# Hybrid trunk on one core: two banks in turn for the weighted values, the head mixes written two slots later, and an end stage laid out anew

## The chip, the core and the metric

The kernel runs on one core of a Trainium2 chip. The core has five engines that work side by side, each through its own list of instructions in order: PE (TensorE, the matrix unit), DVE (VectorE), ACT (ScalarE), POOL (GpSimd) and SP (SyncE, which here issues every DMA transfer). An engine stops where its next instruction waits for another engine or for a transfer, and everything behind that instruction stops with it. The metric is the device time of one execution in microseconds (us); lower is better.

## The reference

Two residual layers on x (2048 tokens by 1024), then an RMSNorm. Layer 0 is gated linear attention. Layer 1, which the change touches, is dilated attention: six heads of width 128, each in three groups with other windows and dilations, mixed by a softmax over the groups' log-sums. Both layers also attend to 256 memory tokens.

```python
for i in range(DEPTH):                                   # DEPTH = 2
    h = rmsnorm(x, norm_w[i])
    mix, q_mem, gate = gla_mixer(...) if i % 2 == 0 else dilated_mixer(h, w_in_b[0])
    mem_o = memory_attention(q_mem, mem_n, w_memkv[i])
    branch = jnp.concatenate([mix, mem_o], axis=-1) * jax.nn.silu(gate)
    x = x + branch @ w_out[i]
return rmsnorm(x, final_norm_w)

# dilated_mixer: DIL_GROUPS = ((128, 1), (512, 4), (2048, 16)), 6 heads of 128
for g, (window, dil) in enumerate(DIL_GROUPS):
    q, k, v = ...                                        # h @ w_in, rope on q and k
    o, lse = dilated_group(q, k, v, window, dil)         # softmax(q k) v, and its log-sum
wts = jax.nn.softmax(jnp.stack(lses, axis=0), axis=0)    # over the three groups
o = jnp.einsum('gbth,gbthd->bthd', wts, jnp.stack(outs, axis=0))
```

## The kernel before

Most operands are split into a high and a low half (two f16 or two fp32r numbers), and the helper `mm3` (lines 180 to 182) multiplies them in three matmuls: L180, L181 and L182 are these three, whoever calls. A tile of PSUM, the memory into which PE writes, is called a bank (128x512 f32). There are eight: `ps_mm` 2, `ps_tr` 2, `ps_g` 2, `ps_o` 1, `ps_x` 1. A pool with two banks hands them out in turn, and a new owner waits until the last reader of the old one is done. `mm_bank` gives out `ps_mm` and `ps_x` in turn.

The attention of layer 1 is a loop over 144 slots (`for s in range(NS)`): 18 units, which are the 6 heads in 3 groups each, by 8 slots. In each slot PE runs, in the order of the program text (`manual_schedule` for PE):

- the scores of slot s-10 into a `ps_g` bank (`att_scores`). DVE masks them and takes the maximum (L1223), DVE makes the exponent's bias (L1227), ACT takes the exponential, POOL splits it in halves, and SP turns the result round by a DMA (`pt<-ph`, L175);
- the weighted values of slot s-13 (`att_pv`, called `pv`): `pt` times `v`. Two slots fill one bank, `ob`; at the next even slot a new one is taken. DVE empties the full bank into `osb` (L1261; into a tile `rw` in the last head);
- the projections of q and k of the next unit (24 matmuls 128x512, `proj_t`). ACT and DVE (L1174, L1175) empty their banks, and every fourth slot the rotary embedding follows, at whose end eight DVE copies (L1193) write q and k, which the scores read.

Once per head, 35 slots after its begin, its three groups are mixed: `att_stats` turns the statistics round (a transpose into `ps_tr`, DVE copy L1275 to `stT`, DMA to `std`), `prep_load` and `prep_mix` work out the mixing weights (`nm`, `dn`; L1299 to L1309) and write them to memory (`fd`). For each of four chunks of 512 tokens `item_og` loads the group outputs (`og`) and the gate (`sg`), `item_fb` loads the weights broadcast to all partitions (`fb`, 768 KB; one tile, so that a chunk's load waits for the mix before), and `item_mix` multiplies and adds (DVE L1341, L1347, L1348, L1350; POOL L1339, L1344) and stores the branch (`brd`, L1352). The weights and values of the next unit (`v<-vd`, 1 MB, L1165) are loaded by the same SP queue.

The end stage is `for x in range(14)`: the last ten slots of scores and thirteen of weighted values, the last gate projection in eight halves (`gate_half`, 12 matmuls 128x512), the mix of head 5 chunk by chunk, and the splits of the output weights and of the branches (`wo_split`, ACT L1427 and DVE L1428). Each of 16 blocks of 128 tokens is then multiplied with the output weights. `load_b` loads and splits a block's seven finished eighths of the branch, `f_main(d, P1)` and `f_main(d, P2)` multiply these with the left and the right 512 columns, `f_fin` adds the eighth that holds head 5 (from `b5s[c]`, the mixed chunk c, which serves blocks 4c to 4c+3) and DVE adds the residual (L1532), which empties the bank. `f_mm` is both one behind the other. Three `f_main` stand inside the end stage: block 0 both sides, block 1 left.

The order of DVE, ACT, POOL and SP is not that of the text: a planner works it out from the dependences when the program is built. PE follows the text here.

Of the kernel before, what the change touches and what calls it, by code (L numbers as in the profile page):

```python
# [35 lines left out]
def trunk(ctx, tc, a, out):  # L36
# [1209 lines left out]
    def att_pv(hd, step):  # L1246
        u, vt = hd["u"], hd["v"]
        pth, ptl, runs = hd["pv"].pop(step)
        j2 = step % 2
        if j2 == 0:  # L1250
            hd["ob"] = bank(ps_o)
        ob = hd["ob"]
        for r_, (kb, sl, n, j) in enumerate(runs):
            x, y = (kb // 4, kb % 4) if u[1] == 0 else (kb % 4, kb // 4)
            cs = slice(sl * P, (sl + n) * P)
            mm3(ob[:, j * P:(j + n) * P], vt[:, x, 0, y], vt[:, x, 1, y], pth[:, cs], ptl[:, cs],
                j2 == 0 and r_ == 0, j2 == 1 and r_ == len(runs) - 1)
        if j2 == 1:
            j4 = step // 2
            osb = tl(*((bk, [P, 512], F32, "rw") if hd["ns"] < 16 and j4 % 2 else (gk, [P, 512], F32, "osb")))  # L1260
            V.tensor_copy(osb, ob)  # L1261
            if hd["ns"] == 16:
                SY.dma_start(o_d[hd["h"]][u[1]][:, j4 * 512:(j4 + 1) * 512], osb)
            else:
                hd["osb"][j4] = osb
# [108 lines left out]
    for s in range(NS):  # L1374
# [31 lines left out]
        if 0 <= h < 5:  # L1406
            step = 4 if h < 4 else 2
            if x == 0:
                att_stats(hds[3 * h + 2], 0)
                preps[h] = prep_load(h)  # L1410
            if x == 1:
                prep_mix(preps.pop(h))
            y, z = divmod(x - 5, step)
            if 0 <= y < 4 and z == 0:
                item_mix(*items.pop(y))
            y, z = divmod(x - 3, step)
            if 0 <= y < 4 and z == 0:
                items[y] = (item_og(h, y), item_fb(h, y))
# [26 lines left out]

    raws = {0: wo_raw(0, tl(stg, [P, KT, 256], F32, "stg"))}
    wo0 = [tl(wp, WSH, F32R, "w") for _ in range(4)]
    its, fbs, pre, b5s = {}, {}, {}, {}
    for x in range(14):
# [4 lines left out]
        c, odd = divmod(x - 4, 2)  # L1454
        if 0 <= c < 4 and not odd:
            att_stats(last, c)
        if x < 8:
            gate_half(x)
# [18 lines left out]
        if x in (5, 6):  # L1477
            ks = slice(4 * (x - 5), 4 * (x - 4))
            wo_split(raws[1][:, ks], wo1[0][:, ks], wo1[1][:, ks])
        if x == 5:  # L1480
# [3 lines left out]
        if x == 7:  # L1484
# [9 lines left out]
            def load_b(p_):  # L1494
                xt = tl(fp, [P, D], F32, "x")
                br = tl(f0, [P, KT - 1, P], F32, "br")
                for k0, k1 in ((0, 5), (6, 8)):
                    o = 0 if k0 == 0 else 5
                    SY.dma_start(br[:, o:o + k1 - k0], br_d[p_ // 4][:, p_ % 4, k0:k1])
                SY.dma_start(xt, x1v[p_])  # L1500
                bhl = tl(f0, [P, 2, KT - 1, P], F32R, ("bhl0", "bhl1")[p_ % 2])
                wo_split(br, bhl[:, 0], bhl[:, 1])
                return dict(p=p_, x=xt, b=bhl, ss=tl(sp, [P, 4], F32, "ss4"), n=0, t={},
# [9 lines left out]
            def f_main(d, parts):  # L1513
                t = mm_bank()
# [39 lines left out]
        if x in (8, 9):  # L1554
            fs[x - 8] = load_b(x - 8)
        if x in (9, 10, 11, 12):
            j, kh = divmod(x - 9, 2)
            ks = slice(4 * kh, 4 * kh + 4)
            wo_split(raws[2 + j][:, ks], *(w[:, ks, j * 256:(j + 1) * 256] for w in wo2))
        if x == 9:  # L1560
            f_main(fs[0], P1)
        if x == 10:
            f_main(fs[1], P1)
        if x == 12:
            f_main(fs[0], P2)
            fs[2] = load_b(2)
    for p_ in range(NB):
        d = fs.pop(p_)
        if p_ > 1:
            f_mm(d, P1)  # L1570
        if p_ + 1 < NB and p_ > 1:
            fs[p_ + 1] = load_b(p_ + 1)
        if p_ == 0:
            f_fin(d, P1)
            f_fin(d, P2)
        elif p_ == 1:
            f_fin(d, P1)
            f_mm(d, P2)
# [5 lines left out]
        f_end(p_, d, D if p_ + 1 < NB else 512)  # L1584

# [54 lines left out]
```

## Time and profile before

| | us |
|---|---|
| median of 3 runs (lowest, highest) | 2668.18 (2666.09, 2670.78) |
| profiled execution, its own time | 2676.5 |
| its span, first to last instruction | 2674.7 |
| PE busy in it | 2532.0 (95%) |
| DVE, ACT, POOL busy | 1610.2, 1342.8, 562.6 |
| mean granted TensorE clock | 0.979 of full speed |

The profiled execution lies 0.31% above the median, and 1.8 us of it lie around the span. PE is busy for all but 142.7 us of the span, so a wait of PE is the thing to look for. In a row of the timeline the first number is the start, the second the length, then engine, line, operation, output and inputs, and in square brackets the idle time of the engine before the instruction and what ended it.

### The profile page before, as it was taken

The page shows a single profiled execution, that of the slowest core. Times are in us where ns is not written, and L with a number is a line of the kernel's source. Part 1 is how long each engine was busy: PE and PEld are TensorE (multiplying, and loading weights), DVE is VectorE, ACT ScalarE, POOL GpSimd, SP SyncE. Part 2 cuts the span into 40 slices and gives each one's busy share as a digit, 9 for nine tenths or more (in the row PEclk, how much of TensorE's full clock was granted, in tenths as well). Part 3 has the DMA queues.
Part 4 walks back from the last instruction along what each step waited for, and adds up shares of the span by engine and source line. Part 5 has one row for each costly group of instructions (what it writes and reads, how often), then busy time and mean ns, then how long its engine had stood idle before and what let it go on. Part 6 is the DMA issues. An engine that isn't in the chain of part 4 may idle for free. (4 is left out here: it accounts for less than half of the span.)

```text
span 2674.7 us, 45223 instructions
## 1 busy us (share of the span) xinstructions
PE 2532.0 (95%) x17137; PEld 1698.7 (64%) x17137; DVE 1610.2 (60%) x3595; ACT 1342.8 (50%) x2957; POOL 562.6 (21%) x471
## 2 busy tenths in 40 slices
PE   7999999899999899999999999899998998987799
PEld 6879999788889644544444455454454544544798
DVE  7445444656866656655645556767767676676543
ACT  6356444544444446556545555454554645545122
POOL 0000000001210134555541122222223222232200
PEclk9999999899999999999999999999999999998899
DMA  6242112334433535777664144654646446476542
GB/s 207 83 130 90 66 52 77 119 101 111 145 97 100 162 124 142 173 171 186 158 171 154 46 87 102 174 140 124 158 116 174 123 118 159 118 172 178 167 155 100
DMA packets 528493, 349.72 MB, mean 131 GB/s; under 512 B 355650, under 2 KB 467732, under 8 KB 525588
## 3 DMA queue, kind: packets, MB, share of 16 engines
q1 hardware_dynamic: 528276, 346.84, 47.5%
q8 instruction: 134, 2.20, 0.3%
q14 instruction: 83, 0.68, 0.1%
HBM read 185.74 MB, written 95.86 MB: 105 GB/s over the span
## 5 line engine op out<-in xcount | busy, mean ns | idle before, releaser
L180 PE MATMUL ps_mm<-h2T,w 128*128 128x512 f16 x1112 | 426.9, 384 | 1.2 <-ACT c L947 1.2
L181 PE MATMUL ps_mm<-h2T,w 128*128 128x512 f16 x1112 | 426.1, 383 | 0.0
L182 PE MATMUL ps_mm<-h2T,w 128*128 128x512 f16 x1112 | 426.0, 383 | 0.0
L180 PE MATMUL ps_mm<-w,hT 128*128 128x256 f16 (+1 forms) x1408 | 389.4, 277 | 3.0 <-DVE ws L123 1.1
L181 PE MATMUL ps_mm<-w,hT 128*128 128x256 f16 (+1 forms) x1408 | 388.4, 276 | 0.0
L182 PE MATMUL ps_mm<-w,hT 128*128 128x256 f16 (+1 forms) x1408 | 387.1, 276 | 0.4 <-DVE hT L384 0.4
L182 PEld LDWEIGHTS <-w 128*128 128x128 f16 x1952 | 192.8, 99 | 237.8 <-issue 12.3
L181 PEld LDWEIGHTS <-w 128*128 128x128 f16 x1952 | 192.9, 99 | 222.8 <-issue 18.5
L180 PEld LDWEIGHTS <-w 128*128 128x128 f16 x1952 | 193.0, 99 | 215.2 <-issue 9.7
L174 POOL TENSOR_TENSOR ph<-pm,ph 128x512 f16<-128x512 f32 (+2 forms) x144 | 144.9, 1006 | 615.2 <-ACT ph L173 429.9
L1232 ACT ACTIVATE pm<-pm,st,cols 128x256 f32<-128x256 f32 (+1 forms) x288 | 156.4, 544 | 172.5 <-DVE st L1227 171.3
L180 PE MATMUL ps_x<-h2T,w 128*128 128x512 f16 x552 | 212.7, 385 | 3.5 <-ACT h2T L701 1.8
L181 PE MATMUL ps_x<-h2T,w 128*128 128x512 f16 x552 | 212.5, 385 | 1.4 <-DVE h2T L702 1.4
L182 PE MATMUL ps_x<-h2T,w 128*128 128x512 f16 x552 | 212.5, 385 | 0.0
L174 POOL TENSOR_TENSOR stg<-mp,stg 128x512 f16<-128x512 f32 x16 | 18.6, 1161 | 753.2 <-DMA ogd<-og 457.3
L180 PEld LDWEIGHTS <-hT 128*128 128x128 f16 x1408 | 139.6, 99 | 24.6 <-issue 5.4
L181 PEld LDWEIGHTS <-hT 128*128 128x128 f16 x1408 | 139.5, 99 | 23.0 <-issue 4.2
L1223 DVE CUSTOM_DVE_ANT_0 pm<-ps_g,mw 128x256 f32<-128x256 f32 (+1 forms) x288 | 93.5, 360 | 99.1 <-PE ps_g L182 98.2
L182 PEld LDWEIGHTS <-hT 128*128 128x128 f16 x1408 | 140.1, 99 | 18.6 <-DVE hT L384 0.7
L1171 ACT ACTIVATE rx<-ps_mm 32x512 f32<-32x512 f32 x96 | 56.2, 585 | 136.8 <-DVE k L1193 89.1
L180 PE MATMUL ps_o<-pt,v 128*128 128x128 f16 (+1 forms) x384 | 76.5, 230 | 48.9 <-DVE osb L1261 43.0
L181 PE MATMUL ps_g<-k,q 128*128 128x256 f16 (+1 forms) x288 | 69.3, 249 | 14.1 <-DVE k L1193 14.1
(463 smaller groups left out, 6034.1 us busy)
## 6 DMA issues: line engine op xcount, KB each, us to landing
stg<-in_w_in_b SPq DMA_DIRECT2D x80, 256.0 KB
v<-vd SPq DMA_DIRECT2D x18, 1024.0 KB
fb<-fd SPq DMA_DIRECT2D x24, 768.0 KB
od<-osb SPq DMA_DIRECT2D x68, 256.0 KB
og<-od SPq DMA_DIRECT2D x68, 256.0 KB
x<-in_x SPq DMA_DIRECT2D x32, 512.0 KB
stg<-in_w_in_b SPq DMA_DIRECT2D x24, 512.0 KB
vd<-vo SPq DMA_DIRECT2D x48, 256.0 KB
```

Of the source, the lines that this page charges most:

```text
L174: G.tensor_tensor(out=lo, in0=src, in1=hi, op=ALU.subtract)
L180: PE.matmul(o, sh, mh, start=first, stop=False)
L181: PE.matmul(o, sh, ml, start=False, stop=False)
L182: PE.matmul(o, sl, mh, start=False, stop=last)
L1171: A.activation(out=X[r0 + 32 * j:r0 + 32 * j + 32, :], in_=ts[j][0:32, :], func=AF.Copy)
L1223: V.tensor_tensor_reduce(out=pm[:, at:at + w * P], in0=s[:, at:at + w * P], in1=masks["mw" if w == 2 else "mf"], scale=1.0, scalar=NEG, op ...
L1232: A.activation(out=p_, in_=p_, func=AF.Exp, scale=sc, bias=st[:, jc + jj:jc + jj + 1], accum_out=st[:, ns + jc + jj:ns + jc + jj + 1])
```

## The change

Three things are done.

1. `att_pv` takes its bank from `ps_o` and from `ps_tr` in turn, instead of always from the one of `ps_o`. `ps_tr` keeps its other users: the transposes of `att_stats` and of `pair_norm`, a norm once per unit.
2. For heads 0 to 3 the calls of `item_og`, `item_fb` and `item_mix` stand two slots later in the text (first load in slot 5 of a head's mix instead of 3, first mix in 7 instead of 5; the step stays 4). For head 4, whose step is 2, nothing changes.
3. In the end stage the gate halves run in steps 0 to 5 (two, two, then one each) instead of 0 to 7. The statistics of head 5 stand one step earlier. The rotary tables, no longer needed, take the branch loads of blocks 0 and 1 from step 1 on (`load_br`). The output weights' splits stand one or two steps earlier, and the split branches of the blocks turn through three tiles. Five `f_main` stand inside the stage instead of three: block 0 left (step 7), block 1 left (9), block 0 right (11) and block 1 right (12) into `ps_g` banks, block 2 left (13). In the closing loop blocks are loaded three ahead.

```diff
--- before.py
+++ after.py
@@ -1248,7 +1248,7 @@
         pth, ptl, runs = hd["pv"].pop(step)
         j2 = step % 2
         if j2 == 0:
-            hd["ob"] = bank(ps_o)
+            hd["ob"] = bank((ps_o, ps_tr)[step // 2 % 2])
         ob = hd["ob"]
         for r_, (kb, sl, n, j) in enumerate(runs):
             x, y = (kb // 4, kb % 4) if u[1] == 0 else (kb % 4, kb // 4)
@@ -1410,10 +1410,10 @@
                 preps[h] = prep_load(h)
             if x == 1:
                 prep_mix(preps.pop(h))
-            y, z = divmod(x - 5, step)
+            y, z = divmod(x - 3 - step, step)
             if 0 <= y < 4 and z == 0:
                 item_mix(*items.pop(y))
-            y, z = divmod(x - 3, step)
+            y, z = divmod(x - 1 - step, step)
             if 0 <= y < 4 and z == 0:
                 items[y] = (item_og(h, y), item_fb(h, y))
 
@@ -1443,6 +1443,11 @@
         if hf == 1:
             gate_silu(gt.pop(c), c)
 
+    def load_br(p_):
+        for k0, k1 in ((0, 5), (6, 8)):
+            o = 0 if k0 == 0 else 5
+            SY.dma_start(brs[p_ % 2][:, o:o + k1 - k0], br_d[p_ // 4][:, p_ % 4, k0:k1])
+
     raws = {0: wo_raw(0, tl(stg, [P, KT, 256], F32, "stg"))}
     wo0 = [tl(wp, WSH, F32R, "w") for _ in range(4)]
     its, fbs, pre, b5s = {}, {}, {}, {}
@@ -1451,11 +1456,20 @@
             scores(NS - 10 + x)
         if x < 13:
             pv(NS - 13 + x)
-        c, odd = divmod(x - 4, 2)
+        if x == 7:
+            f_main(fs[0], P1)
+        if x == 9:
+            f_main(fs[1], P1)
+        for y in ((0, 1), (2, 3), (4,), (5,), (6,), (7,))[x] if x < 6 else ():
+            gate_half(y)
+        c, odd = divmod(x - 3, 2)
         if 0 <= c < 4 and not odd:
             att_stats(last, c)
-        if x < 8:
-            gate_half(x)
+        c, odd = divmod(x - 4, 2)
+        if x == 1:
+            brs = [t[:, 0:(KT - 1) * P].rearrange("p (k n) -> p k n", k=KT - 1) for t in rope]
+            for y in range(2):
+                load_br(y)
         if 0 <= c < 4:
             if not odd:
                 pre[c] = prep_load(5, c)
@@ -1474,14 +1488,14 @@
         if x == 2:
             raws[1] = wo_raw(1, tl(stg, [P, KT, 256], F32, "stg"))
             wo1 = [tl(qp, [P, KT, 256], F32R, nm) for nm in ("q", "k")]
-        if x in (5, 6):
-            ks = slice(4 * (x - 5), 4 * (x - 4))
+        if x in (4, 5):
+            ks = slice(4 * (x - 4), 4 * (x - 3))
             wo_split(raws[1][:, ks], wo1[0][:, ks], wo1[1][:, ks])
-        if x == 5:
+        if x == 4:
             raws[2] = wo_raw(2, tl(vp, [P, KT, 256], F32, "v"))
         if x == 6:
             raws[3] = wo_raw(3, tl(stg, [P, KT, 256], F32, "stg"))
-        if x == 7:
+        if x == 5:
             ch.close()
             f0 = c4.enter_context(pool("f0", 1, "right"))
             fp = c4.enter_context(pool("fp", 3, "right"))
@@ -1491,16 +1505,15 @@
             fw = tl(wp, [P, D], F32, "w")
             SY.dma_start(fw, bcast_row(a["final_norm_w"], D))
 
-            def load_b(p_):
+            bhls = [tl(f0, [P, 2, KT - 1, P], F32R, f"bhl{y}") for y in range(2)]
+
+            def load_b(p_, br=True):
+                if br:
+                    load_br(p_)
                 xt = tl(fp, [P, D], F32, "x")
-                br = tl(f0, [P, KT - 1, P], F32, "br")
-                for k0, k1 in ((0, 5), (6, 8)):
-                    o = 0 if k0 == 0 else 5
-                    SY.dma_start(br[:, o:o + k1 - k0], br_d[p_ // 4][:, p_ % 4, k0:k1])
                 SY.dma_start(xt, x1v[p_])
-                bhl = tl(f0, [P, 2, KT - 1, P], F32R, ("bhl0", "bhl1")[p_ % 2])
-                wo_split(br, bhl[:, 0], bhl[:, 1])
-                return dict(p=p_, x=xt, b=bhl, ss=tl(sp, [P, 4], F32, "ss4"), n=0, t={},
+                wo_split(brs[p_ % 2], bhls[p_ % 3][:, 0], bhls[p_ % 3][:, 1])
+                return dict(p=p_, x=xt, b=bhls[p_ % 3], ss=tl(sp, [P, 4], F32, "ss4"), n=0, t={},
                             e=tl(pk, [P, D], BF16, "pm"))
 
             def wcol(k, lo, c0, n):
@@ -1510,8 +1523,8 @@
                     return wo1[lo][:, k, c0 - 256:c0 - 256 + n]
                 return wo2[lo][:, k, c0 - 512:c0 - 512 + n]
 
-            def f_main(d, parts):
-                t = mm_bank()
+            def f_main(d, parts, t=None):
+                t = mm_bank() if t is None else t
                 d["t"][parts[0]] = t
                 lo_ = parts[0][0]
                 for c0, n in parts:
@@ -1551,37 +1564,35 @@
 
             P1, P2 = [(0, 256), (256, 256)], [(512, 512)]
             fs = {}
-        if x in (8, 9):
-            fs[x - 8] = load_b(x - 8)
-        if x in (9, 10, 11, 12):
-            j, kh = divmod(x - 9, 2)
+        if x in (6, 7):
+            fs[x - 6] = load_b(x - 6, False)
+        if x in (7, 8, 9, 10):
+            j, kh = divmod(x - 7, 2)
             ks = slice(4 * kh, 4 * kh + 4)
             wo_split(raws[2 + j][:, ks], *(w[:, ks, j * 256:(j + 1) * 256] for w in wo2))
-        if x == 9:
-            f_main(fs[0], P1)
         if x == 10:
-            f_main(fs[1], P1)
-        if x == 12:
-            f_main(fs[0], P2)
+            bhls.append(tl(qp, [P, 2, KT - 1, P], F32R, "q"))
             fs[2] = load_b(2)
+        if x in (11, 12):
+            f_main(fs[x - 11], P2, bank(ps_g))
+        if x == 13:
+            f_main(fs[2], P1)
     for p_ in range(NB):
         d = fs.pop(p_)
-        if p_ > 1:
+        if p_ < 3:
+            f_fin(d, P1)
+        else:
             f_mm(d, P1)
-        if p_ + 1 < NB and p_ > 1:
-            fs[p_ + 1] = load_b(p_ + 1)
-        if p_ == 0:
-            f_fin(d, P1)
+        if p_ < 2:
             f_fin(d, P2)
-        elif p_ == 1:
-            f_fin(d, P1)
-            f_mm(d, P2)
         elif p_ + 1 < NB:
             f_mm(d, P2)
         else:
             f_mm(d, [(512, 256)])
             f_mm(d, [(768, 256)])
         f_end(p_, d, D if p_ + 1 < NB else 512)
+        if p_ + 3 < NB:
+            fs[p_ + 3] = load_b(p_ + 3)
 
 
 def _constants():
```

How the change moves instructions shows in the orders of the engines. First PE, at the first bank that changes (unit 0 of the attention, the weighted values `pt` times `v`), as before and after stand against each other:

```order
 L180 LDWEIGHTS v_16646
-L180 MATMUL ps_o_17065<-pt_16900,v_16646 128x128
+L180 MATMUL ps_tr_17065<-pt_16900,v_16646 128x128
 L181 LDWEIGHTS v_16646
-L181 MATMUL ps_o_17065<-pt_16900,v_16646 128x128
+L181 MATMUL ps_tr_17065<-pt_16900,v_16646 128x128
```

The bank is another and the place is the same; the bank after this one is `ps_o` again.

Second DVE, at a mix of head 1 (chunk 2; `fb` the weights, `og` the group outputs, `q` a projection). Before:

```order
L1223 ISA mx_20595 128x1
L1341 TENSOR_TENSOR fb_20861<-og_20857,fb_20861 128x512
L1175 SCALAR_TENSOR_TENSOR q_20420<-ps_mm_20546,q_20420 128x512
L818 TENSOR_SCALAR ws_2895_20580<-ws_2895_20580 128x2
L1227 TENSOR_SCALAR st_2882_20517<-mx_20595,cols_88 128x2
L1347 TENSOR_TENSOR fb_20861<-fb_20861 128x512
```

And after:

```order
L1223 ISA mx_20587 128x1
L1341 TENSOR_TENSOR fb_21002<-og_20998,fb_21002 128x512
L1175 SCALAR_TENSOR_TENSOR q_20412<-ps_mm_20539,q_20412 128x512
L818 TENSOR_SCALAR ws_2895_20573<-ws_2895_20573 128x2
L1227 TENSOR_SCALAR st_2882_20510<-mx_20587,cols_88 128x2
L1347 TENSOR_TENSOR fb_21002<-fb_21002 128x512
```

Nothing moved but the numbers of the tiles: both have the mix of the chunk at row 2266 of DVE. The same holds, but for the bank's name, for every row of PE, DVE, ACT, POOL and SP up to the end stage.

Third DVE in the end stage, at the mix of chunk 1 of head 5 (`rw` holds its weighted values). Before, from the mix's second step on (its first product, L1341, stands four rows above):

```order
L1347 TENSOR_TENSOR fb_26424<-fb_26424 128x512
L1302 TENSOR_TENSOR nm_26474<-mn_26531,nm_26474 16x32 x3
L1348 TENSOR_TENSOR fb_26424<-fb_26424 128x512
L1304 TENSOR_TENSOR dn_26475<-dn_26475,nm_26474 16x3x32
L1350 TENSOR_TENSOR sg_26340<-fb_26424,sg_26340 128x16x32
L1305 TENSOR_TENSOR mn_26531<-dn_26475 16x32
L1306 TENSOR_TENSOR mn_26531<-mn_26531,dn_26475 16x32
L1307 RECIPROCAL mn_26531<-mn_26531 16x32
L1428 TENSOR_TENSOR v_26489<-sg_26340,v_26489 128x512
L1309 SCALAR_TENSOR_TENSOR nm_26474<-nm_26474,cols_88,mn_26531 16x32 x3
L1532 TENSOR_TENSOR x_26492<-ps_mm_26562,x_26492 128x512
```

And after:

```order
L1341 TENSOR_TENSOR fb_26496<-rw_26535,fb_26496 128x512
L1299 TENSOR_TENSOR mn_26635<-nm_26537 16x32
L1261 COPY rw_26756<-ps_tr_26696 128x512
L1300 TENSOR_TENSOR mn_26635<-mn_26635,nm_26537 16x32
L1347 TENSOR_TENSOR fb_26496<-fb_26496 128x512
L1545 TENSOR_TENSOR x_26395<-ps_mm_26430,x_26395 128x512
L1302 TENSOR_TENSOR nm_26537<-mn_26635,nm_26537 16x32 x3
L1545 TENSOR_TENSOR x_26395<-ps_g_26725,x_26395 128x512
L1545 TENSOR_TENSOR x_26498<-ps_x_26586,x_26498 128x512
L1348 TENSOR_TENSOR fb_26496<-fb_26496 128x512
```

The first residual add (L1532 before, L1545 after), which frees a bank for the next block, stood behind the whole mix of chunk 1 and its split (L1428); now it stands behind the first two of the mix's four steps (L1341, L1347) and ahead of the rest.

## Prediction

> **What bounds the kernel now.** I read the page's first parts first: which engine is full, and at which clock.
>
> ```profile
> PE 2532.0 (95%) x17137; PEld 1698.7 (64%) x17137; DVE 1610.2 (60%) x3595; ACT 1342.8 (50%) x2957; POOL 562.6 (21%) x471
> PEclk9999999899999999999999999999999999998899
> ```
>
> PE is busy 95% of 2674.7 us, and its clock falls twice, most at the end. So time is to be won only where PE waits, and where it runs slowly after a wait. The waits of PE over the whole run come next (sum, times, longest):
>
> ```profile
> PE ps_o L180 <- DVE osb L1261: 43.0, 18, 6.1
> PE ps_g L181 <- DVE k L1193: 14.1, 5, 3.5
> ...
> PE ps_x L180 <- ACT bhl L1427: 6.1, 1, 6.1
> PE ps_mm L180 <- ACT bhl L1427: 5.9, 1, 5.9
> PE ps_mm L180 <- DVE x L1532: 4.8, 1, 4.8
> ...
> PE ps_o L180 <- DVE rw L1261: 3.2, 1, 3.2
> PE ps_o L180 <- DMA pt<-ph: 2.7, 3, 1.2
> PE ps_x L182 <- DVE bhl L1428: 2.5, 1, 2.5
> ```
>
> The first row is what part 1 of the change aims at: PE wants the one weighted-value bank before DVE has emptied it. The rows with bhl, x and rw belong to the end stage (part 3). The windows of the end, cut in equal stretches (PE, PEld, DVE, ACT, POOL busy, then clock, DMA share, GB/s):
>
> ```profile
> 2407.23:2474.10 66.87, 49.11 (x323) 31.03 (x322) 45.28 (x118) 39.84 (x90) 15.85 (x15) 0.87 0.66 178
> 2474.10:2541.00 66.90, 53.40 (x333) 47.90 (x333) 40.04 (x75) 12.95 (x31) 14.06 (x8) 0.87 0.58 167
> 2540.97:2607.80 66.83, 66.83 (x435) 60.96 (x434) 27.61 (x37) 19.22 (x48) 0.00 (x0) 1.00 0.47 155
> ```
>
> From 2541 on PE never stops, so the end stage loses 17.8 and 13.5 us by idling in two stretches, some of it at a clock of 0.87.
>
> **Part 1, two banks, in heads 0 to 3.** Why DVE is late with the bank decides what a second one is worth. The timeline around the mix of head 1, DVE and PE together:
>
> ```profile
> 1856.96 2.06 DVE L1341 TENSOR_TENSOR fb<-og,fb 128x512 f32<-128x512 f32 x1 [2.50 <-DMA fb<-fd]
> 1863.38 0.22 PE L180 MATMUL ps_o<-pt,v 128*128 128x128 f16 x1 [1.50 <-DVE osb L1261]
> 1871.95 1.50 DVE L1193 COPY k<-rx 32x512 f16<-32x512 f16 x1
> 1873.51 0.27 PE L181 MATMUL ps_g<-k,q 128*128 128x256 f16 x1 [3.22 <-DVE k L1193]
> 1886.92 1.02 DVE L1341 TENSOR_TENSOR fb<-og,fb 128x512 f32<-128x512 f32 x1 [4.33 <-DMA fb<-fd]
> 1893.50 1.91 DVE L1350 TENSOR_TENSOR sg<-fb,sg 128x512 f32<-128x512 f32 x1
> 1895.43 0.56 SPq L1352 DMA_DIRECT2D brd<-sg  x1
> 1897.08 0.68 DVE L1261 COPY osb<-ps_o 128x512 f32<-128x512 f32 x1
> 1897.21 3.30 SPq L175 DMA_TRANSPOSE pt<-ph  x1
> 1897.81 0.22 PE L180 MATMUL ps_o<-pt,v 128*128 128x128 f16 x1 [3.75 <-DVE osb L1261]
> 1906.16 0.22 PE L180 MATMUL ps_o<-pt,v 128*128 128x128 f16 x1 [0.32 <-DMA pt<-ph]
> ```
>
> DVE stands idle for the weights' transfer (2.50 and 4.33 us), and all that is queued behind L1341 is late: the bank's copy, but also the copies of k and, through the product sg that SP waits for, the next transposing transfer pt. With a second bank PE passes the first wait (1.50) and meets the copy of k, which ends at 1873.45 whatever PE does; the wait of 3.22 becomes 4.72, and nothing is won. At the second wait PE would be 3.75 us earlier, and the slow stretch behind it would go too:
>
> ```profile
> 1897.81:1901.00 3.19, 3.19 (x16) 0.59 0.87 315
> 2394.81:2397.50 2.69, 2.69 (x20) 1.00 1.01 321
> 2412.07:2415.00 2.93, 2.93 (x14) 0.50 0.95 268
> ```
>
> After 3.75 and 4.43 us of waiting PE's clock is 0.59 and 0.50 for some 3 us, which costs some 1.6 us (3.2 us at about half speed); after the 2.52 us at 2394.81 it is 1.00. So PE would reach the next weighted values 5.4 us earlier. But these read the pt issued at 1897.21, behind brd on SP, which waited for DVE's sg (1893.50 + 1.91). It landed only at 1906.1, as the 0.32 us of the last row say. PE would then wait 5.7 us for pt. I price a head at 0 to 1 us, for all four at 1; the ends are -2 (a wait that becomes one long one and then a slower clock) and +6 (pt lands up to 1.5 us a head earlier on a quieter queue).
>
> The clock rule of the Trainium skill ("TensorE: Matmul & The Clock Gate", Part 1: The HAM clock gate) says that half clock comes after a free-running idle window of about 3.4 us and leaves after as much busy time. The rows agree for 3.75 and 4.43 us, and for 2.52. By that rule alone, with waits merged into longer ones, a merged wait would be likelier to bring the slow clock, and part 1 would lose some 1.6 us a head, 6 in all.
>
> The transposes that share `ps_tr` cost nothing here: in PE's order the users of the two banks alternate (norm, values, statistics, values), so that each finds its own bank empty since the slot before.
>
> **Part 2, the mixes.** The planner puts them where they were, on all engines; DVE's wait for fb stays. Price 0, without a cover that could go: no instruction moves.
>
> **Part 1 in head 4.** Its last two waits differ, since no copy of k and no late pt lies behind them:
>
> ```profile
> 2394.81 0.22 PE L180 MATMUL ps_o<-pt,v 128*128 128x128 f16 x1 [2.52 <-DVE osb L1261]
> 2399.84 1.80 SPq L175 DMA_TRANSPOSE pt<-ph  x1
> 2407.93 0.68 DVE L1175 SCALAR_TENSOR_TENSOR q<-ps_x,q 128x512 f16<-128x512 f32 x1
> 2412.07 0.26 PE L180 MATMUL ps_o<-pt,v 128*128 128x128 f16 x1 [4.43 <-DVE osb L1261]
> ```
>
> PE would go on at 2407.64 instead of 2412.07 with pt long issued, and then want the `ps_x` bank, which DVE empties at 2408.61. About 1 us of the 4.43 stays, 3.5 is won; with the slow stretch I take 4, between 1 (DVE slips too) and 6 (all of 4.43 and 1.6). Attention together: 1 + 4 = 5, from -1 to 11 where the ends don't coincide.
>
> **Part 3, the end stage.** Its rows, from the first gate to where PE runs unbroken:
>
> ```profile
> 2421.40 0.38 PE L180 MATMUL ps_mm<-h2T,w 128*128 128x512 f16 x1
> 2447.86 0.75 DVE L309 SCALAR_TENSOR_TENSOR sg<-ps_mm,cols,rx 128x512 f32<-128x512 f32 x1 [4.12 <-DMA sgd<-sg]
> 2479.70 1.01 DVE L1341 TENSOR_TENSOR fb<-osb,fb 128x512 f32<-128x512 f32 x1 [3.56 <-DMA fb<-fd]
> 2496.04 1.05 DVE L1341 TENSOR_TENSOR fb<-rw,fb 128x512 f32<-128x512 f32 x1 [7.17 <-DMA fb<-fd]
> 2499.67 0.67 DVE L1347 TENSOR_TENSOR fb<-fb 128x512 f32<-128x512 f32 x1
> 2504.19 0.67 DVE L1532 TENSOR_TENSOR x<-ps_mm,x 128x512 f32<-128x512 f32 x1
> 2504.92 0.80 PE L180 MATMUL ps_mm<-wh,bhl 128*128 128x512 f32 x1 [4.83 <-DVE x L1532]
> 2667.99 0.28 PE L182 MATMUL ps_mm<-wh,v 128*128 128x256 f32 x1
> 2668.31 0.42 DVE L1532 TENSOR_TENSOR x<-ps_mm,x 128x256 f32<-128x256 f32 x1 [2.45 <-PE ps_mm L182]
> ```
>
> PE resumes 83.5 us after the first gate and works 163.4 us to the last matmul, on 29 halves of blocks (block 1 right, blocks 2 to 15 both sides): 5.63 us each. The tail of 6.4 us stays. After the change PE has block 1 right and block 2 left done but for their quick ends when it comes to the same point: 2 x 5.63 = 11.3 us less behind it. That is won if the point itself is no later. The point hangs on a chain that is not PE's: statistics, weights, fb of chunk 1 (7.17 us of idle DVE), then DVE down to the first residual add. The add stood 8.15 us behind L1341 (2496.04 to 2504.19), behind the whole mix and its split. Now it stands right behind L1347, which began 3.63 us after L1341: 2499.67 + 0.67 = 2500.34, 3.85 us earlier. The fb load itself hangs on the mixing weights of chunk 0 and 1, whose statistics stand a step earlier but with more gates ahead; I take a gain of 2 us there, between -7 and +3. So PE resumes 83.5 - 3.85 - 2 = 77.6 us after the first gate.
>
> More work of PE (two `f_main`, seven eighths of 5.63 each, 9.9 us) now lies ahead of that point. It fits: PE waits 6.1 + 5.9 + 4.8 + 3.2 + 2.5 us there, 22.5 us by the rows above. The branches load from step 1 on, so the waits for their split (bhl, 14.5 us) go as waits for a transfer; what is late next is the chain of weights. The earlier weight splits and loads move past nothing but each other on SP: four branch loads and two weight loads, at 0.3 to 0.6 us of issue, 2 us at most, counted in the range. New waits: transposes and values share `ps_tr` in steps 4, 7 and 9; PE waits there some 1.5 us each, covered by the same slack. The end gains 3.85 + 2 + 11.3 = 17, between 8 (chain 7 later) and 19.
>
> **The sum.** 5 + 17 = 22 us. Against the profiled execution's own time that is 2676.5 - 22 = 2654.5; that execution lies 8.3 us over the median of the runs, so against it 2668.2 - 22 = 2646. A change under 0.2% (5.3 us) could not be told from none.
>
> **The rivals.** *Every wait for the bank vanishes.* For it: 43.0 us in 18 waits, and a slower clock after the long ones. It would be true if k and pt were late because of PE. Against it stand the rows of 1871.95 and 1897.21. Half of the 43 us, with half of the slow stretches (some 12 by 1.6 us), and the end: 2668.2 - 21.5 - 9.6 - 17 = 2620; all of it, 2589. Chance 0.12.
>
> *The chain of weights rules the end.* Chunk 1's fb comes as late as the extra splits push it: at 83.5 us or later PE resumes where it did, and only the 11.3 us, less the lateness, is left. With 4 us late: 2668.2 - 5 - 7 = 2656. For it: DVE's idle 7.17 us there is a wait for a transfer which PE's order does not shorten. Chance 0.22.
>
> *Slower: the shared bank couples PE to the statistics' transfers.* In the end stage PE's transpose waits for a copy on DVE, which is queued behind waits for transfers such as the 4.12 us at 2447.86; the gates, scores and values behind it on PE wait too, and so the statistics of the next chunk. It decides once it costs over 22 us, five such waits of 4.4. Six of 4.12 would be 24.7 and give 2671. Against it: there are three such places, and the chain has slack for PE. Chance 0.05, beside 0.02 for no difference.
>
> **How the numbers follow.** Forecast 0.59, the rivals 0.12, 0.22, 0.05, none 0.02. Faster by over 0.2% are the first three cases, 0.93; same 0.02, slower 0.05. The range reaches from 2630 (the ends 11 and 19 of the sum, 2638, and part of the first rival) to 2664 (the second rival with attention at -1 or the chain 7 late: 2668.2 + 1 - 8 = 2661).
>
> **What would show it.** In the changed kernel's profile: osb waits of PE under 10 us in the attention, but the waits for k (14.1) and pt (2.7) grown to 25 or more together; DVE's idle time for fb unchanged; no wait of PE for bhl; the first residual add (L1545 now) within 5 us of chunk 1's L1341; PE unbroken from about 78 us after the first gate. It is wrong if k and pt are not the next to be late, or if fb of chunk 1 lands elsewhere than 75 us after the first gate.

## The result, and the profile after

| | us |
|---|---|
| before, median of 5 runs | 2668.18 (2666.09 to 2672.55) |
| after, median of 5 runs | 2655.69 (2652.65 to 2657.10) |
| ratio, 95% interval | 0.9949 (0.9935 to 0.9964) |
| profiled execution after: its own time, span | 2655.69, 2653.7 |

The change makes the kernel faster by 12.5 us on the medians; the ratio's interval says 10 to 17 us. The forecast was 2646 in 2630 to 2664: the sign and the range hold, the size was put at 22 us. Between the two profiled executions lie 20.8 us, because that of before was 8.3 us over its median and that of after is on it.

The page's rows of load and clock, after:

```profile
PE 2524.5 (95%) x17137; PEld 1696.6 (64%) x17137; DVE 1607.6 (61%) x3595; ACT 1343.0 (51%) x2957; POOL 565.5 (21%) x471
PEclk9999999999999999999999999999999998999999
```

PE is busy 95% as before. The waits of PE over the whole run, after (sum, times, longest):

```profile
PE ps_o L180 <- DMA pt<-ph: 26.1, 6, 5.7
PE ps_g L180 <- DVE k L1193: 16.4, 5, 4.4
PE ps_g L181 <- DVE k L1193: 15.2, 5, 3.5
...
PE ps_tr L1272 <- ACT pm L1232: 5.5, 2, 3.2
...
PE ps_tr L180 <- DMA pt<-ph: 3.0, 2, 2.8
...
PE ps_mm L180 <- DVE x L1545: 2.7, 1, 2.7
```

The 43.0 us for osb are gone from the list, and so are the rows for bhl and rw. But pt has grown from 2.7 to 29.1 us and k from 15.7 (14.1, and 1.6 in a second row) to 31.6. Added up between 1640 us and the first gate, PE waited 57.5 us before and 57.1 after. The timeline around the mix of head 1 again, DVE, PE and SP together:

```profile
1855.42 2.06 DVE L1341 TENSOR_TENSOR fb<-og,fb 128x512 f32<-128x512 f32 x1 [2.74 <-DMA fb<-fd]
1868.43 0.27 PE L180 MATMUL ps_g<-k,q 128*128 128x256 f16 x1 [2.84 <-DVE k L1193]
1870.64 1.50 DVE L1193 COPY k<-rx 32x512 f16<-32x512 f16 x1
1872.20 0.37 PE L181 MATMUL ps_g<-k,q 128*128 128x256 f16 x1 [3.49 <-DVE k L1193]
1885.28 1.02 DVE L1341 TENSOR_TENSOR fb<-og,fb 128x512 f32<-128x512 f32 x1 [3.44 <-DMA fb<-fd]
1891.86 1.97 DVE L1350 TENSOR_TENSOR sg<-fb,sg 128x512 f32<-128x512 f32 x1
1893.86 0.55 SPq L1352 DMA_DIRECT2D brd<-sg  x1
1896.18 2.49 SPq L175 DMA_TRANSPOSE pt<-ph  x1
1904.48 0.27 PE L180 MATMUL ps_o<-pt,v 128*128 128x128 f16 x1 [4.99 <-DMA pt<-ph]
```

This is the picture of before with other names on PE's rows. DVE idles for fb at the same two places. PE passes the bank without a wait (1.50 us before) and stops at k for 2.84 and 3.49 us instead of 0.80 and 3.22, then at pt for 4.99 us instead of 3.75 at the bank and 0.32 at pt. DVE's own idle time for fb between 1500 and 2400 us hardly changed (36.3 us after, 40.0 before):

```profile
DVE fb L1341 <- DMA fb<-fd: 36.3, 10, 4.8
```

The end stage, after: the first gate, chunk 1 of head 5 on DVE, and where PE begins to run unbroken; then the window between the two (PE, PEld, DVE, ACT, POOL busy, clock, DMA share, GB/s):

```profile
2414.61 0.38 PE L180 MATMUL ps_mm<-h2T,w 128*128 128x512 f16 x1
2437.00 0.38 PE L1272 MATMUL ps_tr<-ident,st 128*8 128x128 f32 x1 [3.21 <-ACT pm L1232]
2489.37 1.06 DVE L1341 TENSOR_TENSOR fb<-rw,fb 128x512 f32<-128x512 f32 x1 [4.44 <-DMA fb<-fd]
2492.97 0.67 DVE L1347 TENSOR_TENSOR fb<-fb 128x512 f32<-128x512 f32 x1
2493.58 0.67 DVE L1545 TENSOR_TENSOR x<-ps_mm,x 128x512 f32<-128x512 f32 x1
2494.30 0.54 PE L180 MATMUL ps_mm<-wh,q 128*128 128x512 f32 x1 [2.71 <-DVE x L1545]
2646.91 0.28 PE L182 MATMUL ps_mm<-wh,v 128*128 128x256 f32 x1
```

```profile
2414.61:2494.30 79.69, 67.93 (x457) 51.02 (x455) 52.24 (x129) 38.93 (x80) 21.98 (x16) 0.94 0.74 202
```

PE is unbroken from 79.7 us after the first gate (83.5 before) and then works 152.6 us (163.1). From the first gate to the last matmul it is 232.3 us, against 246.6 before. PE waits 11.8 us in that time, against 26.8, so its busy time is the same within 1 us, and what was won is time spent waiting.

### The profile page after: what moved, and what is told of

The parts are those of the page before. It is cut to its first block, busy times and chain, and to the rows that moved or that the text cites. A ratio compares the mean times of both kernels' runs of the same rounds, so it can differ in the third digit from the quotient of the medians.

```text
span 2653.7 us, 45228 instructions
## 1 busy us (share of the span) xinstructions
PE 2524.5 (95%) x17137; PEld 1696.6 (64%) x17137; DVE 1607.6 (61%) x3595; ACT 1343.0 (51%) x2957; POOL 565.5 (21%) x471
## 4 chain that ended last, share of the span: by engine, by line
PE 69%; DMA 9%; DVE 9%; issue 5%; ACT 4%; POOL 2%; SPq 2%; DVEq 0%; ACTq 0%; POOLq 0%
PE ps_mm L180 13%; PE ps_mm L181 13%; PE ps_mm L182 13%; PE ps_x L181 5%; PE ps_x L182 5%; PE ps_x L180 5%; DMA fb<-fd 2%; DMA pt<-ph 1%; PE ps_tr L167 1%; PE ps_o L180 1%; PE ps_o L182 1%; PE ps_o L181 1%; DMA stg<-in_w_in_b 1%; PE ps_g L180 1%; PE ps_g L554 1%
## 5 line engine op out<-in xcount | busy, mean ns | idle before, releaser
L182 PEld LDWEIGHTS <-w 128*128 128x128 f16 x1952 | 192.3, 99 | 236.1 <-issue 9.1
L180 PE MATMUL ps_x<-h2T,w 128*128 128x512 f16 x552 | 210.3, 381 | 3.4 <-ACT h2T L701 2.0
L181 PE MATMUL ps_x<-h2T,w 128*128 128x512 f16 x552 | 210.4, 381 | 1.4 <-DVE h2T L702 1.4
L182 PE MATMUL ps_x<-h2T,w 128*128 128x512 f16 x552 | 210.1, 381 | 0.0
L180 PEld LDWEIGHTS <-hT 128*128 128x128 f16 x1408 | 138.9, 99 | 24.1 <-issue 5.4
L181 PE MATMUL ps_g<-k,q 128*128 128x256 f16 (+1 forms) x288 | 70.6, 254 | 15.2 <-DVE k L1193 15.2
L180 PE MATMUL ps_g<-k,q 128*128 128x256 f16 (+1 forms) x288 | 69.0, 253 | 16.4 <-DVE k L1193 16.4
```

The costliest lines, as they stand in the source:

```text
L180: PE.matmul(o, sh, mh, start=first, stop=False)
L181: PE.matmul(o, sh, ml, start=False, stop=False)
L182: PE.matmul(o, sl, mh, start=False, stop=last)
```

## The experiments

All ratios are to the kernel before, measured beside it on the same chip, with their 95% intervals. The experiments ran on three chips, on which the kernel before had medians of 2670.5, 2677.0 and 2676.0 us, so that ratios are compared, not times.

For each kernel's profile the time was also cut in three at the same instructions of PE: from the first weighted values to those of head 5 (the mixes of heads 0 to 3 lie in it), from there to the first gate (the mix of head 4), and from the first gate to the last matmul. Each row is one profile. Two pairs of rows run one and the same order of instructions: before and p2_mixes, and after and late_br (shown below). Between the rows of a pair the ratios differ by up to 0.002, the first stretch by 1.2 us, the second by 1.7 and the end by 3.2, so smaller differences tell nothing.

| kernel | ratio | heads 0-3, us | head 4 | end |
|---|---|---|---|---|
| before | 1 | 810.0 | 87.9 | 246.6 |
| p2_mixes | 1.0004 (0.9995 to 1.0012) | 808.8 | 86.2 | 245.7 |
| p3_end | 0.9963 (0.9950 to 0.9976) | 808.5 | 86.3 | 237.6 |
| p1_banks | 0.9971 (0.9963 to 0.9980) | 808.1 | 81.8 | 241.2 |
| after | 0.9949 (0.9935 to 0.9964) | 810.6 | 83.1 | 232.3 |
| late_stats | 0.9927 (0.9912 to 0.9943) | 810.1 | 81.0 | 233.5 |
| three_main | 0.9941 (0.9922 to 0.9960) | 813.3 | 82.7 | 235.4 |
| late_br | 0.9928 (0.9914 to 0.9942) | 809.8 | 82.1 | 235.5 |
| pin_early | 0.9925 (0.9908 to 0.9941) | 806.8 | 81.6 | 238.7 |
| pin_y0 | 0.9832 (0.9819 to 0.9846) | 783.8 | 80.5 | 233.9 |
| pin_after | 0.9808 (0.9796 to 0.9821) | 774.8 | 81.6 | 236.1 |
| pin_nobank | 0.9817 (0.9802 to 0.9832) | 772.9 | 80.9 | 242.6 |
| best | 0.9798 (0.9784 to 0.9811) | 775.4 | 73.5 | 240.7 |
| best_v | 0.9821 (0.9808 to 0.9835) | 782.4 | 68.4 | 246.2 |

**Each part alone.** First the banks.

```diff
-            hd["ob"] = bank(ps_o)
+            hd["ob"] = bank((ps_o, ps_tr)[step // 2 % 2])
```

> The kernel before with the two banks in turn alone. Theory A (DVE waits for the weights fb, and what is queued behind is late; a second bank only lets PE meet the next late thing): about 2664, 4 us less than before, all of it in head 4; in heads 0 to 3 the waits for the bank (some 40 us) turn into waits for k and pt of the same sum; the end stage gives nothing. Theory B (the banks are what the changed kernel gains by): 2656, the whole 12 us.

Measured 0.9971, about 8 us, between the two theories. In heads 0 to 3 nothing (808.1 against 808.5 to 810.0 with one bank); the waits moved as expected:

```profile
PE ps_o L180 <- DMA pt<-ph: 17.5, 4, 5.2
PE ps_g L181 <- DVE k L1193: 12.8, 4, 3.3
PE ps_g L180 <- DVE k L1193: 12.0, 4, 3.5
```

These are PE's first waits between 1250 and 2330 us; osb is not among them. Head 4 gives 5 us. What neither theory had: the end stage gives 5 as well (in one profile), although its layout is that of before. The waits for osb and rw there (1.5 and 3.2 us before) shrink to 0.8, and PE runs unbroken 80.2 us after the first gate instead of 83.5.

Then the mixes, in the text alone:

```diff
-            y, z = divmod(x - 5, step)
+            y, z = divmod(x - 3 - step, step)
...
-            y, z = divmod(x - 3, step)
+            y, z = divmod(x - 1 - step, step)
```

> The kernel before with the mixes written two slots later alone. Its instructions stand in the same order as before on every engine, so both theories expect 2668 within the noise, and a profile like that of before. It also shows how much two profiles of one and the same order differ: if the 8 us by which the profiled execution of before lay above its median were chance, this one's span is nearer to 2666.

Measured 1.0004: no change, as the order said. Its profile has a span of 2670.4 us, 4.3 less than that of before with the same order, of which 2.9 lie in the attention, 0.9 in the end stage and 0.6 ahead of both. So two profiles of one order differ by several us in the very places of the change.

Then the end stage alone (the rest of the diff):

> The kernel before with the end stage laid anew alone. Theory A: 2656 to 2660 (8 to 12 us less), with the waits for bhl gone and PE unbroken from about 80 us after the first gate. Theory B: 2667, since the chain of weights through fb of chunk 1 sets the end in either layout.

Measured 0.9963, about 10 us, with 8.6 of them in the end stage; no wait for bhl is left. Theory A, though PE is not unbroken from 80 us: it still waits 1.1 us at 82.1 and 2.6 us at 118.5 us after the first gate. The two parts add up within the intervals: 8 and 10 us alone, 10 to 17 together.

**The root.** The mix's first DVE instruction is tied to the one written before it, so that the planner can no longer draw it forward. This makes the later place in the text take effect.

```diff
+        p0 = V.tensor_tensor(out=fb[:, 0], in0=o0.rearrange("p (l q) -> p q l", q=16),
+                             in1=fb[:, 0], op=ALU.mult)
+        if osb is None:
+            tc.keep_in_program_order(p0)
```

> The changed kernel, but with the first DVE product of each mix (heads 0 to 4) pinned behind the DVE instruction written before it, so that the mixes really come later in DVE's order. Theory A: DVE's idle time for fb falls from 36 us to under 10, the waits of PE for k and pt in the attention fall from 57 us to under 15, and with the slow stretches behind them the time is 2605 to 2620. Theory C (k and pt are late because DVE and SP are full around the mix, wherever it stands): the waits stay above 40 us, 2645 to 2660.

Measured 0.9808, 51 us under the kernel before. The size is theory A's, though not every wait went. DVE's idle time for fb (1500 to 2400 us), then PE's first waits between 1250 and 2330 us:

```profile
DVE fb L1341 <- DMA fb<-fd: 9.0, 2, 4.7
```

```profile
PE ps_tr L180 <- DMA pt<-ph: 17.7, 4, 5.4
PE ps_g L180 <- DVE k L1193: 4.9, 1, 4.9
PE ps_g L181 <- DVE k L1193: 3.1, 1, 3.1
```

The waits for k that are left are those of head 4, whose mixes stay in their old place; in heads 0 to 3 there are none. Those for pt are smaller but did not go: 17.7 us, at another pair of slots. Heads 0 to 3 take 774.8 us instead of 810.6. Of these 35.8 us, 27.4 are idle time of PE that went (45.1 to 17.7); the rest is shorter busy time, at a mean granted clock of 0.985 instead of 0.971.

With the pinned mixes, part 1 undone (one bank again):

> The kernel with pinned mixes, with the weighted values always in the one bank of ps_o again (part 1 undone). Theory A (DVE was late only for its wait for fb): without that wait the bank is emptied in time, no waits for osb over 5 us in the attention, and the time stays within 5 us of that with the pinned mixes (2620). Theory B (the second bank is what hides DVE's lateness): waits for osb of 20 us or more come back and the time is 2635 or more.

Measured 0.9817 against 0.9808, intervals overlapping: theory A. Waits for the bank came back, but small ones, PE between 1250 and 2330 us:

```profile
PE ps_o L180 <- DMA pt<-ph: 14.0, 4, 4.0
PE ps_o L180 <- DVE osb L1261: 8.2, 4, 4.1
```

Of the 8.2 us, 5.1 lie in head 4. Heads 0 to 3 are no slower with one bank (772.9). So once DVE is in time the second bank buys nothing there. The end stage is 6.5 us longer without it (242.6 for 236.1), which goes with the 5 us that the banks alone gave there.

With the pinned mixes, part 2 undone (two slots earlier):

> The kernel with pinned mixes, with the mixes of heads 0 to 3 written two slots earlier again (part 2 undone). If the distance from the load of fb to its mix is what counts, it is as long as before (the load starts when the mix before ends, either way four slots earlier), so 2615 to 2628, with DVE's wait for fb under 15 us. If the place in the head counts (beside the norm, the rope and the loads of the next unit), 2635 or more.

Measured 0.9925: almost all of the gain is lost, so the place in the head counts. DVE's wait for fb is down, yet k is as late as ever:

```profile
DVE fb L1341 <- DMA fb<-fd: 16.9, 6, 4.1
```

```profile
PE ps_g L181 <- DVE k L1193: 13.6, 4, 3.7
PE ps_g L180 <- DVE k L1193: 11.1, 4, 3.6
```

The first mix of head 1 still begins in front of the copies of k, after its wait for fb:

```profile
1858.50 2.06 DVE L1341 TENSOR_TENSOR fb<-og,fb 128x512 f32<-128x512 f32 x1 [3.04 <-DMA fb<-fd]
1873.57 1.51 DVE L1193 COPY k<-rx 32x512 f16<-32x512 f16 x1
```

My reading that the distance from load to mix was what counts is wrong for the first chunk: its fb follows the mixing weights, and no earlier mix holds the load up. Its pinned place two slots earlier is the very place that the planner had chosen. So what counts should be whether the first mix stands ahead of the copies. That was tried by pinning the first mix alone, in the changed kernel:

```diff
+        if osb is None and c == 0:
+            tc.keep_in_program_order(p0)
```

> The changed kernel with only the first of a head's four mixes pinned behind the DVE instruction written before it. If PE waits for k because DVE waits for the first chunk's fb ahead of the copies of k, the k waits (24 us in heads 0 to 3 of the changed kernel) go although three mixes stand where they were, and the ratio to the kernel before is 0.984 to 0.989. If all four mixes are needed, 0.992 or more.

Measured 0.9832, more than expected: 0.0117 under the changed kernel (31 us), where pinning all four gives 0.0141 (38 us), though three of four mixes stay where the planner likes. (Against late_br, which was measured on the same chip and runs the changed kernel's order, it is 0.0096.) PE's waits for k between 1250 and 2330 us, first in the changed kernel:

```profile
PE ps_g L181 <- DVE k L1193: 12.1, 4, 3.5
PE ps_g L180 <- DVE k L1193: 12.0, 4, 3.3
```

and the waits with the first mix pinned:

```profile
PE ps_tr L180 <- DMA pt<-ph: 9.2, 7, 2.8
PE ps_g L180 <- DVE mx L1223: 7.4, 6, 2.2
...
PE ps_g L181 <- DVE k L1193: 1.2, 2, 0.9
```

24.1 us of waits for k have become 1.5 (0.3 of them in a row not shown). DVE still waits 25.4 us for fb in this kernel, so its idle time costs where PE's next input is queued behind it. What the pin moves is the whole mix: its wait for fb (2.74 us in head 1 of the changed kernel), its own steps, and with them the products of POOL that run beside the copies of k and lengthen them (last section). The runs don't tell these apart.

**The end stage taken apart.** Two of the five partial products are put back behind the stage:

```diff
-        if x in (11, 12):
-            f_main(fs[x - 11], P2, bank(ps_g))
-        if x == 13:
-            f_main(fs[2], P1)
+        if x == 11:
+            f_main(fs[0], P2, bank(ps_g))
```

> The changed kernel with three early partial products instead of five (block 1 right and block 2 left are computed after the stage). Theory A: the point at which PE runs unbroken stays at 78 to 80 us after the first gate and 11 us more work lies behind it: 2664 to 2668. Rival (without them PE reaches the chain's end no later and the first blocks' adds come sooner): 2656 to 2660.

Measured 0.9941 against 0.9949: not theory A, and no loss that could be told, where the rival allowed some. The end stage takes 235.4 us against 232.3 and 235.5 in the two profiles of the changed order, so the two products are worth 0 to 3 us and not 11. PE's last waits in that kernel are for chunk 0's split values v, and from there it runs unbroken, long before the mix of chunk 1 begins:

```profile
2492.04 0.39 PE L180 MATMUL ps_mm<-w,v 128*128 128x256 f32 x1 [1.63 <-ACT v L1427]
2493.18 0.39 PE L182 MATMUL ps_mm<-w,v 128*128 128x256 f32 x1 [0.64 <-DVE v L1428]
2501.25 1.08 DVE L1341 TENSOR_TENSOR fb<-rw,fb 128x512 f32<-128x512 f32 x1 [1.36 <-DMA fb<-fd]
```

That is 69.7 us after its first gate (2423.49), ten us sooner than in the changed kernel, and 165.7 us of work lie behind it instead of 152.6. Work taken from ahead of the point moved the point too. Chunk 1, at 77.8 us, held nothing up here.

The early branch loads, written later in the text (blocks 0 and 1 load their branches with `load_b`, in steps 6 and 7):

> The changed kernel with the branch loads of blocks 0 and 1 moved from step 1 of the end stage to steps 6 and 7, beside their splits. If the 14 us of waits for bhl that went were won by the early loads, they come back and the ratio rises by 0.003 to 0.005, to 0.998 to 1.000. If the chain of weights sets the end anyway, the ratio stays at 0.993 to 0.996.

Measured 0.9928, no loss; but nothing was undone. By operation and tile name every engine runs the changed kernel's order, row for row: the planner issued the loads as early as it had before the edit. Here are the first branch load and the longest wait for one, in the kernel before; then the first load in the changed kernel and in this one:

```profile
2459.73 0.35 SPq L1499 DMA_DIRECT2D br<-brd  x1
2480.94 0.95 ACT L1427 ACTIVATE bhl<-br 128x896 fp32r<-128x896 f32 x1 [9.94 <-DMA br<-brd]
```

```profile
2418.53 0.38 SPq L1449 DMA_DIRECT2D rope<-brd  x1
2424.46 0.38 SPq L1449 DMA_DIRECT2D rope<-brd  x1
```

After the first gate these loads stand at 38.3 us before, 3.9 in the changed kernel and 5.5 here. So this run doesn't say what the early loads are worth; it is a second measurement of the changed kernel. The traces say this much: in the kernel before ACT stood 2.23 and 9.94 us for the branches that it was to split, while PE waited for the split bhl; in the changed kernel the loads are issued 34 us sooner and the first splits run without a wait, 31.9 us after the first gate. That fits the early loads as what won the 14.5 us. But the splits of the weights, the gates and the block loads moved as well, and no run took the early loads alone away.

The statistics of head 5 back in their old step:

```diff
-        c, odd = divmod(x - 3, 2)
+        c, odd = divmod(x - 4, 2)
```

> The changed kernel with the statistics of head 5 one step later, where they stood before. If the 5.5 us in which PE waits for ACT's exponentials (pm) at the transpose are a cost of that move, they go and PE is unbroken 2 to 4 us sooner: 2652 to 2654. If the chain of weights sets the end, the later start of it costs its step: 2656 to 2660.

Measured 0.9927 (0.9912 to 0.9943), beside 0.9949 (0.9935 to 0.9964), and 233.5 us of end stage beside 232.3. The wait for the exponentials goes, waits of 2.3 us for stT and 4.2 for x come. The time is below what either case expected, yet not told apart from that of the changed kernel: the step is worth nothing either way that could be told. The mix of chunk 1 began 80.2 us after the first gate instead of 74.8, and the end stage grew by only 1.2: four residual adds now stood ahead of that mix on DVE.

**Towards a better version.** `best` is the pinned kernel with `late_stats` and with the mixes of head 4 one slot later:

> The kernel with pinned mixes, with the statistics of head 5 one step later and the mixes of head 4 one slot later. Expected from its waits: 8 us of waits for k in head 4 and 9 us for ACT's exponentials in the end stage, of which half is won: ratio 0.976 to 0.980. If both waits only move, 0.981.

Measured 0.9798 (0.9784 to 0.9811) beside 0.9808 (0.9796 to 0.9821): not told apart. Head 4 gained 8 us and the end stage lost 4.6: the last mix of head 4 now begins 18 us after the first gate. Both pinned versions beat the kernel before, by 1.9 to 2.0%, and the changed one, by 1.4 to 1.5%.

`best_v` is `best` with one more tie:

```diff
-        SY.dma_start(vt, v_d[u[0], u[1], i])
+        tc.keep_in_program_order(SY.dma_start(vt, v_d[u[0], u[1], i]))
```

> The same, with the 1 MB load of v also pinned behind the SP transfers written before it, so that the eight transfers of the statistics (std) stand ahead of it on SP. With the pinned mixes SP stood 7.6 us at them behind v and fb, and the transposing transfers pt behind them were late (17.7 us of PE's waits). If that is the cause, about 10 us go: ratio 0.972 to 0.977. If pt is late for the traffic on the transfer engines, whatever the order on SP, no change against the kernel without this.

Measured 0.9821, no gain but rather a loss: its four runs took 2625.4 to 2631.0 us, those of `best` beside it 2617.5 to 2623.7. The statistics' transfers did come ahead of v, but SP still stood 5.2 us at them, behind fb:

```profile
1934.48 0.62 SPq L1332 DMA_DIRECT2D fb<-fd  x1
...
1936.24 5.24 SPq L1283 DMA_DIRECT2D std<-stT  x8
```

So the test took away only part of what it should have. In this head the transposing transfer behind them went out at 1943.92, as soon as POOL's split ph was done, so there SP was no longer what held it; PE still waited 3.3 us for it. Why pt is late with pinned mixes stays open.

## Why the prediction was right, and where its sizes were off

**Part 1, heads 0 to 3: right in mechanism, and in size within the noise.** Forecast: the wait moves to k and pt, 1 us. In the five kernels with two banks and unpinned mixes (p1_banks, after, late_stats, three_main, late_br) this stretch takes 808.1 to 813.3 us, mean 810.4; in the three with one bank 808.5 to 810.0, mean 809.1. No gain. Where the prediction had 4.72 us at k and 5.7 at pt, the trace has 3.49 behind an earlier 2.84, and 4.99. The root, the first mix standing with its wait for fb ahead of the copies, was shown by pin_after and pin_y0; how much of it is the wait and how much the mix's own work was not shown. The loss of 6 us which the Trainium skill's clock rule ("TensorE: Matmul & The Clock Gate", Part 1: The HAM clock gate) would have brought by itself is not there beyond the spread, though the slow clock follows the new wait as it did the old (first row below): PE's busy time in this stretch is 764.7 us on average with one bank and 765.1 with two. The three rows with which the prediction found the 3.4 us to agree are not all: in the same profile of before, waits of 2.46 and 2.58 us at 1709.63 and 2371.74 were followed by clocks of 0.67 and 0.68 as well (second row for the first of them):

```profile
1904.48:1907.70 3.22, 3.22 (x15) 0.53 1.16 310
1709.63:1712.50 2.87, 2.87 (x15) 0.67 0.06 12
```

**Part 1, head 4: right.** Forecast 4; 86.8 us on average with one bank, 82.1 with two: 4.7.

**Part 2: right.** Price 0, measured 1.0004.

**Part 3: too high, and for a reason that was half wrong.** Forecast 17; measured 14.3 between the two profiles, and 12.3 between the mean of before and p2_mixes and that of after and late_br. The add that no longer stands behind the whole mix came as forecast: 4.21 us behind L1341 instead of 8.15. The 2 us for an earlier chain were wrong: chunk 1's product began 74.8 us after the first gate, as it had before (74.6). That the work behind the point would shrink by 11 us was right as a count (152.6 us for 163.1), but not as a cause: three_main shows that PE's own work ahead of the point had filled the time, so that the two products are worth 0 to 3. The waits for bhl went, as forecast; that the early loads did it was not shown. And some 5 us of the end stage belong to the banks (p1_banks, pin_nobank), which the prediction had costed only in the attention.

**The sum.** Forecast 22. The stretches give 3.4 (4.7 - 1.3) in the attention and 12.3 in the end stage, 15.7. The ratio of the changed kernel gives 13.6 with 9.5 to 17.3, that of late_br, the same order, 19 with 15 to 23. So 22 was too high by some 3 to 8 us. The terms that were mis-sized are the gain of the chain (2, measured 0) and the two products (11.3, measured 0 to 3); against them stands the gain of the banks in the end stage (put at nothing, measured about 5). Besides, a gain summed in one profile of before was subtracted from the median: that profile's attention and end stage were 3.7 us longer than those of p2_mixes, which runs the same order, so some of what was counted as gain may have been chance.

**The rivals.** *Every wait vanishes* did not come with the second bank, but with the pinned mixes the waits for k went in heads 0 to 3 and those for pt shrank: k was not late because of PE, and not by nature either. *The chain rules the end* forecast 2656, next to the 2655.7 measured, but that is luck: PE resumed 3.8 us sooner than before, and in late_stats and three_main chunk 1 came later (80.2 and 77.8 us) without holding the end up. *Slower* did not show: the transposes waited 5.5 us for ACT's exponentials, which was not among the new waits named, and not for DVE's copies.

## What to carry to other kernels

A second buffer takes its user only as far as the next late input: first find out what the emptying engine was waiting for, and what else is queued behind that wait, for that is what the consumer meets next. Where a planner sets the order, moving lines in the text may move no instruction (here in p2_mixes, and in late_br, whose test was empty for that reason); compare the engines' orders, and if an instruction that waits for a transfer stands ahead of urgent ones, tie it behind them (here one tie on the first mix of each head was worth 1.0 to 1.2% beyond the change). And cut a profile in stretches at fixed instructions: over eight profiles with the mixes in one place these told 4.7 us in head 4 from none in heads 0 to 3, where two spans of one order differed by 4 us.

## What the runs showed of the hardware that was not expected

**Copies on DVE that met an instruction of POOL ended only after it.** Of the 248 copies of L1193 between 1500 and 2330 us of the changed kernel 222 take 0.27 to 0.29 us, but 26 take 0.72 to 1.51. Each of these 26 overlaps an instruction of POOL and ends 0.14 to 0.15 us after the end of one. The copy of k at 1870.64, shown further up with 1.50 us, runs beside the first of these rows; the copy behind it, when POOL is done, takes 0.28:

```profile
1870.44 1.56 POOL L1344 TENSOR_TENSOR fb<-og,fb 128x512 f32<-128x512 f32 x1
1872.18 0.28 DVE L1193 COPY q<-rx 32x512 f16<-32x512 f16 x1
```

That copy of k and the copy before it (1.19 us) took 2.1 us longer than the short ones, of the 3.49 us for which PE then waited for k. No run moved POOL's products alone.

**Small transfers stand behind large ones, by a wait that the program holds.** SP, which issues all transfers, itself stood still for 5 to 8 us at eight transfers of 2 KB (`std`), where their issue alone takes 0.2 to 0.5 us each. The waits of SP between 1640 and 2370 us of pin_after name large loads ahead of them, not `stT`, as what it waited for:

```profile
SPq L1283 <- DMA v<-vd: 9.3, 4, 2.5
...
SPq L1283 <- DMA fb<-fd: 7.1, 4, 2.0
```

The semaphores in the trace say why. The 1264 transfers of SP use eight semaphores strictly in turn, and most issues (994 in pin_after) first wait on the one that they will use, that is, for the transfer eight issues before to land. In head 1 the sixth `std` went out at 1928.76, when fb, issued at 1923.18, had landed, and the seventh at 1931.51, when v had. So no limit of the queue was measured here. And with fb still among the eight issues ahead, moving v alone (best_v) could not end the wait.
